# A lockstep top-k search with three tiles on ScalarE, and a pooling input of its own for each half, in a one-core hybrid encoder layer

## The chip, the cores and the metric

The kernel runs on one core of a Trainium2 chip. The metric is the device time of one execution in microseconds. A measured time is the median of several runs; the profile is of one further execution. Engines are named as in the profile: PE (matrix engine; PEld its weight loads), ACT, DVE, POOL, and SP, which here only issues DMAs.

## The reference, cut to what matters

```python
h = rmsnorm(x, norm_g)                      # 1024 tokens, 1024 channels
z = h @ w_in                                # one projection for everything below
# A, pooling: per group of 64 channels a trailing mean over 2/4/8/16 tokens, minus the token
p = win_sum / cnt - v;  a = (p @ w_grp) * scale * silu(pg)
# B, sparse attention: an indexer picks 256 keys for each query
score = sum_h iw[q,h] * relu(iq[q,h] . ik[s]);  score = -inf beyond the query's chunk of 64
sel = top_k(score, 256);  b = softmax(q . k[sel] / 8) @ v[sel] * silu(dg)
# C, forgetting attention: causal, with the bias F[t] - F[s], F = cumsum(log_sigmoid(ff + bf))
c = softmax(q . k / 8 + F[t] - F[s]) @ v * silu(fg)
x = x + concat(a, b, c) @ w_out;  return rmsnorm(x, final_g)
```

## The kernel before, in words

Tokens are cut into 8 tiles of 128. Every float32 product is made of three matmuls on a high and a low part (`mm3`, its matmuls on line 457). `norm` and `idx_proj` make the transposed activations and the indexer's columns tile by tile; `idx_k` makes the indexer's keys, high parts by ACT (line 560) and low parts on partitions 32 to 63 and 96 to 127 by two DVE subtractions (line 562). `idx_tile` makes the scores of tiles 2 to 7 (`sc2` to `sc7`; tile i has (i+1)*128 keys; tiles 0 and 1 have no more than 256 keys and need no search).

The projections that follow are jobs of 24 matmuls, and they are what PE always has at hand. A "half" is 128 output columns for 512 tokens (`chan`, 24 matmuls of 512 columns): fk and fq (keys and queries of C), gp (gate of A), POOL (the pooling input v), gf (gate of C), dk, dq (B) and gd (gate of B). The jobs fv and dv are 384 columns for one token tile (`tokproj`, 24 matmuls of 384 columns). Each job fills one PSUM tile `pj`, of which there are three, and PE can begin a fourth job only when the first has been read out: fk, fq, dk, dq by ACT on line 718 and DVE on 719, fv and dv by ACT 659 and DVE 660, gates by ACT 732 (tanh) and DVE 734, POOL by ACT 1042 into the buffer v.

`pool_tile(m)` runs twice. Its v and two sum buffers s1, s2 come from one ring `pq` of three; windows are added on POOL (line 1049, copy 1053), DVE forms the means (1065, 1067, 1069), PE multiplies (1073), DVE scales the result into a tile `th` (1077), which is stored to DRAM (`mx_p`). The ring `th` has two tiles, which the gates use too (line 731), each stored (`gt_f`) before it is used again.

The top 256 of a row are found by a search for the threshold, bit by bit: a first count and 31 steps, each a count of the scores below the trial value and three small instructions that set the next one (786, 788, 789). Tiles 6 and 7 are counted on ACT (Sign with a summing output, line 768), tiles 2 to 5 on DVE (line 772); the two searches run apart, each with small instructions of its own. `finish` turns thresholds into masks on DVE (813 to 843; with `fix` a tile is counted twice). Until finish has let go of its row buffers there is no place for the attention's tiles `P`, so the first of C's score evictions (line 929) stands behind it.

The order on every engine is made ahead of time by `Plan.schedule`, a list scheduler with planned durations and priorities; each engine then takes its instructions strictly in that order. SP issues all DMAs, in one such order too: loads of keys and queries for the attention (`load_k`, `load_q`) stand in line with stores.

## Time and profile before

| | |
|---|---|
| time, median of 3 runs | 678.64 us (677.1 to 679.01) |
| the profiled execution's own time | 675.91 us |
| its span, first to last instruction | 674.1 us |
| mean granted TensorE clock | 0.983 |
| busy: PE, DVE, ACT, POOL | 631.3, 524.4, 395.9, 202.5 us |

The own time is 1.8 us more than the span. Shares of busy time are means over stages that differ: the indexer up to 135 us, the search with projections up to 293 us, attention with projections up to 600 us, and the output projection.

### The profile page before, as it was taken

How to read it: one execution, taken by the hardware profiler on the slowest of the kernel's cores; microseconds unless marked ns; L12 is line 12 of the kernel's file. 1: busy time of each engine (PE TensorE's matmuls, PEld its weight loads, DVE VectorE, ACT ScalarE, POOL GpSimd, SP SyncE). 2: the span in 40 equal slices, each digit the busy share in tenths (PEclk: the TensorE clock that was granted, in tenths of full speed). 3: DMA queues.
4: the chain of work that ended last, by engine and by line, in shares of the span. 5: the costliest groups of instructions: out<-in, count | busy, mean ns of one | idle time of the engine just before them, and what ended most of it. 6: DMA issues, size and time to landing. Idle time of an engine off the chain costs nothing. (4 is left out here: it accounts for less than half of the span.)

```text
span 674.1 us, 10707 instructions
## 1 busy us (share of the span) xinstructions
PE 631.3 (94%) x3278; PEld 529.4 (79%) x3278; DVE 524.4 (78%) x1363; ACT 395.9 (59%) x904; POOL 202.5 (30%) x218
## 2 busy tenths in 40 slices
PE   7899999999999399879999899999899999989995
PEld 5798777799888399667878688888778777778884
DVE  5978999999999989989997666758576868655322
ACT  5745777566666545531658467778567869731211
POOL 3610324520036512114442442512031435132311
PEclk9999999999999699989999999999899999999999
DMA  7707554640035323744647668569874555266211
GB/s 227 222 1 199 152 167 110 184 132 3 16 97 138 84 104 106 220 144 135 209 156 236 188 171 236 180 189 276 227 233 151 184 175 172 64 196 202 103 63 62
DMA packets 98439, 103.02 MB, mean 153 GB/s; under 512 B 10983, under 2 KB 67399, under 8 KB 98382
## 3 DMA queue, kind: packets, MB, share of 16 engines
q1 hardware_dynamic: 98382, 102.34, 50.8%
q8 instruction: 26, 0.43, 0.3%
q14 instruction: 31, 0.25, 0.1%
HBM read 72.35 MB, written 29.96 MB: 152 GB/s over the span
## 5 line engine op out<-in xcount | busy, mean ns | idle before, releaser
L457 PE MATMUL bank<-RA 128*128 128x512 f32 (+2 forms) x2016 | 492.0, 381 | 16.5 <-ACT FA L1042 10.5
L457 PEld LDWEIGHTS bank<-RA 128*128 128x128 f32 x2016 | 361.2, 190 | 67.6 <-ACT FA L1042 10.9
L957 ACT ACTIVATE RA<-bank 128x512 fp32r<-128x512 f32 (+3 forms) x144 | 67.8, 488 | 62.9 <-PE bank L950 58.8
L772 DVE TENSOR_SCALAR_CACHE_REDUCE FA<-FA 128x384 bf16<-128x384 f32 (+3 forms) x128 | 103.4, 808 | 1.6
L690 POOL TENSOR_TENSOR RA<-FA,RA 128x512 fp32r<-128x512 f32 x44 | 63.8, 1461 | 126.8 <-ACT RA L689 122.0
L768 ACT ACTIVATE FA<-FA 128x896 bf16<-128x896 f32 x64 | 69.8, 1090 | 52.6 <-DVE FA L789 42.9
L929 DVE CUSTOM_DVE_ANT_0 FA<-bank,FA 128x512 f32<-128x512 f32 (+3 forms) x144 | 77.4, 552 | 28.5 <-PE bank L921 9.9
L959 DVE TENSOR_TENSOR RA<-bank,RA 128x512 fp32r<-128x512 f32 (+3 forms) x144 | 77.0, 553 | 23.1 <-ACT RA L957 14.0
L940 ACT ACTIVATE FA<-FA 128x512 f32<-128x512 f32 (+3 forms) x144 | 86.8, 607 | 7.3 <-DVE FA L935 7.2
L950 PE MATMUL bank<-FA 128*128 128x128 f32 x432 | 79.4, 276 | 3.2 <-DVE RA L959 2.2
L950 PEld LDWEIGHTS bank<-FA 128*128 128x128 f32 x432 | 55.7, 141 | 21.3 <-DVE RA L959 5.3
L918 PE MATMUL bank<-RA 128*128 128x512 f32 (+3 forms) x144 | 52.3, 365 | 6.0 <-DVE FA L929 2.9
L602 DVE SCALAR_TENSOR_TENSOR FA<-FA 128x512 f32<-128x512 f32 (+3 forms) x70 | 54.2, 798 | 1.9
L921 PE MATMUL bank<-RA 128*128 128x512 f32 (+3 forms) x144 | 51.1, 361 | 2.6 <-DMA RA<-qk_dq 2.4
L965 PE MATMUL bank<-RA 128*128 128x512 f32 (+3 forms) x144 | 53.4, 375 | 0.0
L963 PE MATMUL bank<-RA 128*128 128x512 f32 (+3 forms) x144 | 49.2, 342 | 0.5 <-ACT RA L957 0.5
L594 ACT ACTIVATE FA<-bank 128x512 f32<-128x512 f32 (+3 forms) x80 | 39.7, 527 | 16.3 <-DVE FA L602 6.8
L925 POOL TENSOR_TENSOR FA<-FA 128x128 f32<-128x128 f32 x48 | 25.6, 541 | 71.2 <-DMA FA<-nf_d 34.9
L918 PEld LDWEIGHTS bank<-RA 128*128 128x128 f32 x144 | 27.1, 189 | 13.3 <-DVE FA L929 7.7
L921 PEld LDWEIGHTS bank<-RA 128*128 128x128 f32 x144 | 27.3, 191 | 6.2 <-DMA RA<-qk_dq 2.6
L963 PEld LDWEIGHTS bank<-RA 128*128 128x128 f32 x144 | 27.3, 190 | 6.3 <-ACT RA L957 2.1
L997 POOL TENSOR_TENSOR FA<-FA 128x512 f32<-128x512 f32 x12 | 16.2, 1347 | 52.9 <-DVE FA L993 27.6
(145 smaller groups left out, 688.1 us busy)
## 6 DMA issues: line engine op xcount, KB each, us to landing
FA<-in_w_in_dram SPq DMA_DIRECT2D x60, 256.0 KB, 3.4
FA<-in_x_dram SPq DMA_DIRECT2D x15, 512.0 KB, 3.6
RA<-qk_fq SPq DMA_DIRECT2D x48, 128.0 KB, 3.9
RA<-qk_dq SPq DMA_DIRECT2D x48, 128.0 KB, 2.8
RA<-qk_dk SPq DMA_DIRECT2D x36, 128.0 KB, 3.3
FA<-in_w_out_dram SPq DMA_DIRECT2D x16, 256.0 KB, 2.8
out_dram<-FA SPq DMA_DIRECT2D x7, 512.0 KB
RA<-qi SPq DMA_DIRECT2D x24, 128.0 KB, 3.0
```

The lines of the kernel that those rows point to most:

```text
L457: M(lambda: nc.tensor.matmul(p()[:, :n], fa(), fb(), start=st, stop=sp), n, keys, [p], pr)
L690: G(lambda raw=raw, s=s: nc.gpsimd.tensor_tensor(Wl()[:, s, :], raw(), f32(Wh()[:, s, :]), op=OP.subtract), 512, [raw, (Wh, kh)], [(Wl, kh ...
L768: A(lambda c=c, i=i, jk=jk, s=s: nc.scalar.activation(jk(), SC[i](), AF.Sign, bias=s(), scale=-1.0, accum_out=cn()[:, c:c + 1]), n, sck(i) ...
L772: V(lambda c=c, i=i, jk=jk, s=s: nc.vector.tensor_scalar(jk(), SC[i](), s(), None, op0=OP.is_lt, op1=OP.add, accum_out=cn()[:, c:c + 1]), ...
L918: M(lambda s=s, k=k, n=n, j=j, hd=hd: nc.tensor.matmul(s()[:, :n], qx()[:, hd, j * 128:j * 128 + 128], k()[:, hd, :n], start=True, stop=Fa ...
L921: M(lambda s=s, k=k, n=n, j=j, hd=hd: nc.tensor.matmul(s()[:, :n], ql()[:, hd, j * 128:j * 128 + 128], k()[:, hd, :n], start=False, stop=T ...
L929: V(lambda s=s, Pt=Pt, n=n, u=u, j=j, mx=mx, bias=bias: nc.vector.tensor_tensor_reduce(Pt()[:, :n], s()[:, :n], bias()[:, u * 512:u * 512 ...
L940: A(lambda Pt=Ps[j][u], n=n, j=j, u=u, hd=hd, nm=nm: nc.scalar.activation(Pt()[:, :n], Pt()[:, :n], AF.Exp, bias=nm()[:, j:j + 1], accum_o ...
L950: M(lambda pt=pt, j=j, Pt=Ps[j][kb // 4], c=kb % 4 * 128: nc.tensor.transpose(pt()[:, j * 128:j * 128 + 128], Pt()[:, c:c + 128], ident()) ...
L957: A(lambda ph=ph, pt=pt, c=c: nc.scalar.activation(ph()[:, c], pt()[:, c], AF.Copy), n, [pt], [ph], pr, psum=True)
L959: V(lambda ph=ph, pl=pl, pt=pt, c=c: nc.vector.tensor_tensor(pl()[:, c], pt()[:, c], f32(ph()[:, c]), op=OP.subtract), n, [pt, ph], [pl], pr)
L963: M(lambda o=o, v=v, ph=ph, c=c, kb=kb: nc.tensor.matmul(o()[:, c], v(), ph()[:, c], start=(kb == 0), stop=False), n, kv + [ph], [o], pr)
```

## The change

- One `search` for all six tiles: tiles 5, 6, 7 are counted on ACT, tiles 2, 3, 4 on DVE, and one set of small instructions on six columns sets all trial values, so all counts of a step wait for the slowest of the step before. `finish` follows for all tiles, with the fix for 5, 6 and 7.
- Each `pool_tile` has a v of its own (tag `pv`, two buffers); the ring `pq` holds only the sums.
- The two small evictions of `idx_proj` (lines 540 and 542) go from DVE to ACT; the bias is added once for all tiles in `forget`.
- `idx_k` makes the low parts with one DVE instruction on all partitions, with a per-partition factor 0 or -1 (`lom`).
- 24 extra small matmuls (`keep_warm`) are queued at the lowest priority, behind the first tile's transposes.

```diff
-    lay("F", f1 + 9 * KB, [("pq", 4160, 3), ("pw", KB, 1)], 1)
+    lay("F", f1 + 9 * KB + 4160, [("pq", 4160, 2), ("pw", KB, 1)], 1)
+    P.tag("pv", "F", 4160, [FSZ - 4160, f1 + 9 * KB], 1)
...
+    def keep_warm(i):
+        for q in range(24):
+            P.op(PE, lambda q=q: nc.tensor.matmul(wu()[:, q % 4 * 128:q % 4 * 128 + 128], identb(), identb(), start=True,
+                                                  stop=True), 0.107, [k_identb, (hT[0], i, 0, "h")], [(wu, q % 4)], 100)
...
-        V(lambda: nc.vector.tensor_tensor(FFA()[:, i * NH:i * NH + NH], p()[:, 296:302], bfb(), op=OP.add), 6,
-          [p, k_bfb], [(cc, "ff", i)], pr)
-        V(lambda: nc.vector.tensor_scalar(iwb()[:, 8 * i:8 * i + 8], p()[:, 288:296], 8.0 ** -0.5, None, op0=OP.mult),
-          8, [p], [(cc, "iw", i)], pr)
+        A(lambda: nc.scalar.activation(FFA()[:, i * NH:i * NH + NH], p()[:, 296:302], AF.Copy), 6, [p],
+          [(cc, "ff", i)], pr, psum=True)
+        A(lambda: nc.scalar.activation(iwb()[:, 8 * i:8 * i + 8], p()[:, 288:296], AF.Copy, scale=8.0 ** -0.5), 8, [p],
+          [(cc, "iw", i)], pr, psum=True)
...
-        for r in (32, 96):
-            V(lambda r=r: nc.vector.tensor_tensor(kk()[r:r + 32], pk()[r:r + 32, :128], f32(kk()[r:r + 32]),
-                                                  op=OP.subtract), 128, [pk, (KI, i)], [(KI, i)], pr)
+        V(lambda: nc.vector.scalar_tensor_tensor(kk(), f32(kk()), lom(), pk()[:, :128], op0=OP.mult, op1=OP.add), 128,
+          [pk, (KI, i), k_lom], [(KI, i)], pr)
...
-        v, s1, s2 = (P.new("pq", [128, W]) for _ in range(3))
+        v, s1, s2 = P.new("pv", [128, W]), P.new("pq", [128, W]), P.new("pq", [128, W])
...
-    sa = search([6, 7], "a")
-    sv = search([2, 3, 4, 5], "v")
-    finish([2, 3, 4, 5], *sv, False)
-    finish([6, 7], *sa, True)
+    on_act = [5, 6, 7]
+    tiles = on_act + [2, 3, 4]
+    finish(tiles, on_act, *search(tiles, on_act))
```

Since the scheduler decides the order, three places show what it made of this. Line numbers of the changed kernel are its own.

ACT at the pooling input: L1042 (L1054 in the changed kernel) evicts a POOL half from a PSUM bank, L768 (L777) is a search count, L689 (L699) a weight split, L659 (L669) the eviction of a dv job. Before:

```order
L768 ACTIVATE FA<-FA 128x896
L768 ACTIVATE FA<-FA 128x1024
L768 ACTIVATE FA<-FA 128x896
L768 ACTIVATE FA<-FA 128x1024
L689 ACTIVATE RA<-FA 128x512 x2
L1042 ACTIVATE FA<-bank_66 128x512
L1042 ACTIVATE FA<-bank_65 128x512
L659 ACTIVATE RA<-bank_71 128x3x2x64
```

Of the change:

```order
L1054 ACTIVATE FA<-bank_71 128x512
L777 ACTIVATE FA<-FA 128x768
L777 ACTIVATE FA<-FA 128x896
L777 ACTIVATE FA<-FA 128x1024
L777 ACTIVATE FA<-FA 128x768
L1054 ACTIVATE FA<-bank_66 128x512
L699 ACTIVATE RA<-FA 128x512 x2
L777 ACTIVATE FA<-FA 128x896
L777 ACTIVATE FA<-FA 128x1024
L669 ACTIVATE RA<-bank_65 128x3x2x64
```

The two evictions of the second pooling half stood together before; they now stand four counts apart, and a step has three counts on ACT instead of two.

ACT at the first gates of C: L732 (L742) is a gate's tanh out of a PSUM bank, L768 (L777) a count. Before:

```order
L768 ACTIVATE FA<-FA 128x1024
L768 ACTIVATE FA<-FA 128x896
L732 ACTIVATE FA<-bank_65 128x512
L768 ACTIVATE FA<-FA 128x1024
L732 ACTIVATE FA<-bank_71 128x512
L732 ACTIVATE FA<-bank_66 128x512
```

Of the change:

```order
L777 ACTIVATE FA<-FA 128x768
L777 ACTIVATE FA<-FA 128x896
L742 ACTIVATE FA<-bank_66 128x512
L777 ACTIVATE FA<-FA 128x1024
L742 ACTIVATE FA<-bank_65 128x512
L777 ACTIVATE FA<-FA 128x768
L777 ACTIVATE FA<-FA 128x896
L742 ACTIVATE FA<-bank_71 128x512
L777 ACTIVATE FA<-FA 128x1024
L699 ACTIVATE RA<-FA 128x512 x2
L742 ACTIVATE FA<-bank_66 128x512
L777 ACTIVATE FA<-FA 128x768
```

Before, one count stood behind the first gate; now seven do (five of them in these rows, two more below), which are all of the last two steps and the last count of the one ahead of them.

DVE where the attention begins: L929 (L941) is C's score eviction, named ISA here, L813 (L825) counts in finish, L734 (L744) and L719 (L729) are evictions of a gate and of a dk half. Before:

```order
L813 TENSOR_SCALAR FA<-FA 128x768
L841 SCALAR_TENSOR_TENSOR FA<-FA 128x640
L832 TENSOR_SCALAR FA<-FA 128x1
L835 TENSOR_SCALAR FA<-FA 128x768
L734 SCALAR_TENSOR_TENSOR FA<-FA,bank_71 128x512
L843 TENSOR_SCALAR FA<-FA 128x640
L837 SCALAR_TENSOR_TENSOR FA<-FA 128x768
L929 ISA FA<-bank_67,FA 128x512
```

Of the change:

```order
L825 TENSOR_SCALAR FA<-FA 128x768
L847 TENSOR_SCALAR FA<-FA 128x768
L729 SCALAR_TENSOR_TENSOR RA<-bank_65,RA 128x512
L844 TENSOR_SCALAR FA<-FA 128x1
L849 SCALAR_TENSOR_TENSOR FA<-FA 128x768
L825 TENSOR_SCALAR FA<-FA 128x896
L941 ISA FA<-bank_67,FA 128x512
```

The gate ahead of the first score eviction was the fifth half of gf; now the second half of dk is evicted ahead of it, so three more projection halves (gf's sixth, two of dk) stand in front of the attention.

## Rows read from the trace of the kernel before

**Rows 1.** Page, busy time, share of the span and instructions of each engine.

```profile
PE 631.3 (94%) x3278; PEld 529.4 (79%) x3278; DVE 524.4 (78%) x1363; ACT 395.9 (59%) x904; POOL 202.5 (30%) x218
```

**Rows 2.** Waits of PE alone: who waited for whom, us, times, longest.

```profile
PE bank L457 <- ACT FA L1042: 10.5, 1, 10.5
PE bank L457 <- DVE FA L734: 3.8, 1, 3.8
...
PE bank L918 <- DMA RA<-qk_fq: 2.0, 1, 2.0
```

**Rows 3.** Timeline, 205 to 250 us: start, duration, instruction, idle before and its releaser.

```profile
220.10 1.05 POOL L1053 COPY FA<-FA 64x1024 f32<-64x1024 f32 x1
...
228.79 1.98 DVE L1065 SCALAR_TENSOR_TENSOR FA<-FA 128x1024 f32<-128x1024 f32 x1
...
232.16 1.09 ACT L1042 ACTIVATE FA<-bank 128x512 f32<-128x512 f32 x2 [3.29 <-DVE FA L789]
...
232.81 15.71 PE L457 MATMUL bank<-RA 128*128 128x384 f32 x75 [10.55 <-ACT FA L1042]
```

**Rows 4.** Windows of 2 us: engines' busy time, then granted clock, DMA share, GB/s.

```profile
230.00:232.00 2.00, 0.00 (x0) 0.00 (x0) 2.00 (x5) 0.00 (x0) 1.89 (x1) 0.50 0.54 122
...
236.00:238.00 2.00, 2.00 (x8) 2.00 (x7) 1.96 (x13) 1.13 (x2) 0.00 (x0) 0.50 0.03 12
238.00:240.00 2.00, 2.00 (x12) 2.00 (x12) 0.84 (x2) 0.28 (x1) 0.00 (x0) 0.98 0.00 0
```

**Rows 5.** Windows: one in the fv jobs, one in the output projection.

```profile
150.00:160.00 10.00, 10.00 (x60) 10.00 (x59) 9.89 (x34) 7.14 (x16) 0.00 (x0) 1.00 0.13 33
...
600.00:660.00 60.00, 60.00 (x267) 49.70 (x266) 22.16 (x42) 12.46 (x18) 17.69 (x13) 1.00 0.37 126
```

**Rows 6.** Window in the first stage.

```profile
20.00:40.00 20.00, 17.61 (x127) 16.28 (x126) 18.52 (x49) 12.69 (x28) 11.37 (x13) 1.00 0.51 148
```

**Rows 7.** Instruction groups by form: busy us, mean ns of one, idle before.

```profile
L768 ACT ACTIVATE FA<-FA 128x1024 bf16<-128x1024 f32 x32 | 36.5, 1141 | 4.1 <-POOL FA L605 3.5
L768 ACT ACTIVATE FA<-FA 128x896 bf16<-128x896 f32 x32 | 33.3, 1039 | 48.5 <-DVE FA L789 42.9 <-DVE FA L788 3.9 <-DVE FA L781 1.7
...
L788 DVE TENSOR_TENSOR FA<-FA 128x2 int32<-128x2 f32 x31 | 10.6, 343 | 1.0 <-ACT FA L768 1.0
```

**Rows 8.** Timeline, ACT in two steps of the search.

```profile
225.42 1.04 ACT L768 ACTIVATE FA<-FA 128x896 bf16<-128x896 f32 x1 [3.92 <-DVE FA L789]
...
226.59 1.15 ACT L768 ACTIVATE FA<-FA 128x1024 bf16<-128x1024 f32 x1
...
235.74 0.19 ACT L768 ACTIVATION_READ_ACCUMULATOR FA<-FA 128x1 f32 x1
...
236.44 1.04 ACT L768 ACTIVATE FA<-FA 128x896 bf16<-128x896 f32 x1 [0.51 <-DVE FA L789]
```

**Rows 9.** Timeline, POOL and DVE at 217 us.

```profile
216.88 1.89 POOL L1049 TENSOR_TENSOR FA<-FA 64x1024 f32<-64x1024 f32 x1
...
217.15 1.72 DVE L788 TENSOR_TENSOR FA<-FA 128x2 int32<-128x2 f32 x2
```

**Rows 10.** Timeline, SP, ACT and PE at the first gates of C.

```profile
267.95 2.39 SPq L360 DMA_DIRECT2D RA<-qk_fk  x4
...
287.38 0.45 SPq L360 DMA_DIRECT2D mx_p<-FA  x1
...
290.86 0.60 ACT L732 ACTIVATE FA<-bank 128x512 f32<-128x512 f32 x1 [3.17 <-DMA mx_p<-FA]
...
292.24 2.98 PE L457 MATMUL bank<-RA 128*128 128x512 f32 x7 [3.75 <-DVE FA L734]
```

**Rows 11.** Timeline, DVE from the first finish to the first score eviction.

```profile
286.57 0.61 DVE L813 TENSOR_SCALAR_CACHE_REDUCE FA<-FA 128x384 bf16<-128x384 f32 x1
...
308.85 0.69 DVE L929 CUSTOM_DVE_ANT_0 FA<-bank,FA 128x512 f32<-128x512 f32 x1 [0.28 <-POOL FA L925]
```

**Rows 12.** Windows of the attention, 310 to 600 us: their sum.

```profile
sum 290.00, PE 279.67 PEld 230.33 DVE 214.38 ACT 197.74 POOL 93.65; mean PE 46.61 PEld 38.39 DVE 35.73 ACT 32.96 POOL 15.61
```

More of the change, by code (lines that the diff above doesn't have):

```diff
@@ L310, in tile_trunk @@
     lay("R", 64 * KB, [("mh", 4 * KB, 2), ("ml", 4 * KB, 2)], 4)
-    NC_ = 672
+    NC_ = 680
     f1 = lay("F", 0, [("c", NC_ * 4, 1), ("raw", 2 * KB, 3), ("th", 2 * KB, 2), ("rs", 32, 4), ("ss", 32, 4),
@@ L392, in tile_trunk @@
     bfb, k_bfb = carve(NH)
+    lom, k_lom = carve(1)
     xt0 = P.new("xt", [128, D])
@@ L417, in tile_trunk @@
     G(lambda: nc.gpsimd.memset(half(), -0.5), 1, [], [k_half])
+    for q in range(4):
+        G(lambda q=q: nc.gpsimd.memset(lom()[32 * q:32 * q + 32], -float(q % 2)), 1, [], [k_lom])
     V(lambda: nc.vector.tensor_scalar(cmask(), iot(), 0.0, NEG, op0=OP.is_gt, op1=OP.mult), 128, [k_iot], [k_cmask],
@@ L622, in forget @@
         v = nc.vector
+        V(lambda: v.tensor_tensor(fa().rearrange("p (i h) -> p i h", h=NH), fa().rearrange("p (i h) -> p i h", h=NH),
+                                  bfb()[:, None, :].to_broadcast([128, NT, NH]), op=OP.add), N, kf + [k_bfb], kf, pr)
         V(lambda: v.tensor_scalar(za(), fa(), -1.0, None, op0=OP.mult), N, kf, [ka], pr)
@@ L744, in tile_trunk, with search @@
     mask = [lambda i=i: maskb()[:, moff[i]:moff[i] + (i + 1) * 128] for i in range(NT)]
-    def search(tiles, a):
-        nq = len(tiles)
-        eng = ACT if a == "a" else DVE
+    def search(tiles, on_act):
+        nq, a = len(tiles), "s"
         t0, _ = carve(nq)
@@ L756, in search @@
             n = (i + 1) * 128
-            G(lambda c=c, n=n: nc.gpsimd.memset(th()[:, c:c + 1],
-                                                float(n - 2 * TOPK if eng == ACT else n - TOPK) + 0.5), 1, [],
+            G(lambda c=c, i=i, n=n: nc.gpsimd.memset(th()[:, c:c + 1],
+                                                     float(n - (2 * TOPK if i in on_act else TOPK)) + 0.5), 1, [],
               [k("th")], 0)
@@ L762, in count @@
         def count(t, kt):
-            for c, i in enumerate(tiles):
+            for c, i in sorted(enumerate(tiles), key=lambda x: x[1] not in on_act):
                 n = (i + 1) * 128
                 s = (lambda: 0.0) if t is None else (lambda c=c: t()[:, c:c + 1])
-                jk = P.new("jka" if eng == ACT else "jkv", [128, n], BF)
-                if eng == ACT:
+                if i in on_act:
+                    jk = P.new("jka", [128, n], BF)
                     A(lambda c=c, i=i, jk=jk, s=s: nc.scalar.activation(jk(), SC[i](), AF.Sign, bias=s(), scale=-1.0,
@@ L771, in count @@
                 else:
+                    jk = P.new("jkv", [128, n], BF)
                     V(lambda c=c, i=i, jk=jk, s=s: nc.vector.tensor_scalar(jk(), SC[i](), s(), None, op0=OP.is_lt,
@@ L793, in search, with finish @@
         return cur, kc, cn, a
-    def finish(tiles, t, kt, cn, a, fix):
+    def finish(tiles, on_act, t, kt, cn, a):
         pr = PR_SEL
         v = nc.vector
-        if fix:
-            nz, knz = carve(len(tiles))
-            V(lambda: v.tensor_scalar(nz().bitcast(I32), t().bitcast(I32), 0x7fffffff, None, op0=OP.bitwise_and), 2,
-              [kt], [knz], pr)
-            V(lambda: v.tensor_scalar(nz(), nz(), 2.0 ** -126, None, op0=OP.is_ge), 2, [knz], [knz], pr)
-            V(lambda: v.tensor_tensor(t(), t(), nz(), op=OP.mult), 2, [kt, knz], [kt], pr)
-        for c, i in enumerate(tiles):
+        na = len(on_act)
+        nz, knz = carve(na)
+        ta = lambda: t()[:, :na]
+        V(lambda: v.tensor_scalar(nz().bitcast(I32), ta().bitcast(I32), 0x7fffffff, None, op0=OP.bitwise_and), na,
+          [kt], [knz], pr)
+        V(lambda: v.tensor_scalar(nz(), nz(), 2.0 ** -126, None, op0=OP.is_ge), na, [knz], [knz], pr)
+        V(lambda: v.tensor_tensor(ta(), ta(), nz(), op=OP.mult), na, [kt, knz], [kt], pr)
+        for c, i in sorted(enumerate(tiles), key=lambda x: x[1]):
+            fix = i in on_act
             n = (i + 1) * 128
@@ L1163, in tile_trunk @@
         norm(i)
+        if i == 0:
+            keep_warm(0)
         idx_proj(i, Wi)
```

2 lines of the change are left out of this document (1 added, 1 removed).

## The prediction

> **What bounds the kernel now.** I read the busy shares first: PE works 631.3 of 674.1 us [rows 1], so the question is where the other 42.8 us lie, and how much of it this change can reach. PE's own waits answer the first half [rows 2]: one wait of 10.5 us on a pooling eviction, one of 3.8 on a gate, one of 2.0 on a key load. DVE with 524 us and ACT with 396 [rows 1] are not the bound by their sums, but in the fv jobs DVE is busy 9.89 of 10 us while PE is busy all of them [rows 5], so the search fills DVE there and its small instructions decide when other work on DVE comes.
>
> The long wait is read from the timeline [rows 3]. PE restarts at 232.81 after 10.55 us idle, when ACT runs two evictions L1042 together at 232.16. These wait for their target, v of the second pooling half, and v has the place of a buffer of the first half, whose last reader on DVE begins with L1065 at 228.79. POOL's last sum for it was done at 221.15, so DVE, in order behind search counts, added 7.6 us. Meanwhile three finished `pj` tiles stood unread. The idle time cost clock too: it is 0.50 in the stall and still 0.50 at 236 to 238, 0.98 after [rows 4]. Those are the two levels 1.2 and 2.4 GHz; 5.2 us of work at the lower one (232.8 to 238) cost 2.6 us. The whole is 13.1 us.
>
> **Pooling buffers of its own.** With `pv`, the second v waits for nothing in the first half. All 13.1 us come back, if PE then finds its evictions on time. It does if the search, which shares ACT and DVE with them, keeps pace.
>
> **The search against PE.** A 512-column matmul takes 60.0/267 = 0.225 us, a half 5.4 us; a 384-column one 10.0/60 = 0.167, an fv or dv job 4.0 us [rows 5]. From fq's last pair of halves to the end of the third gf half PE has 13 halves and 16 such jobs, 134 us, and four L1073 in full float32, which I put at four 512-column matmuls each, 0.9 us (an estimate): 138 us.
>
> A step of the new search on ACT: from a 896 count to the next count 1.17 us, from the start of the 1024 count 1.05 us to its read-out, and from a read-out to the next step's first count 0.70 [rows 8]. A 768 count isn't shown on ACT; 1024 against 896 is 0.10 us more [rows 7], so I take 1.17 less 0.10, 1.07 (bounds: the fit could be off by 0.1). Together 3.99 us, 31 times 124 us. Evictions that stand at a step's end lie inside the 0.70. From the changed order some 23 evictions and splits stand between counts of one step and add about 0.5 us each, 12 us, and pairs of splits 2 us more.
>
> DVE counted four tiles a step and ran two sets of small instructions; with three tiles and one set it no longer sets the pace. But its small instructions now stand in ACT's path. L788 takes 343 ns on average [rows 7], and the reason is visible: two of them that began at 217.15 ended at 218.87, with POOL's addition that began at 216.88 and ended at 218.77 [rows 9]. Some 0.18 us each for L788 and 0.1 for L789 (an estimate by the same excess), 31 times, is 9 us. So the search takes about 147 us, and its first step begins when PE's first half of this stretch is done and read out.
>
> The Trainium skill, in "SBUF — State Buffer", section "SBUF: two separate sides", says that DVE and GpSimd share a port pair as an exclusive lock, held for a whole instruction. Rows 9 agree. By that rule every step whose small instructions meet a POOL addition is lengthened by up to all of it; what that would give is the last rival below.
>
> PE ends the last dv job about 120 us from its start; the 25 steps ahead of that job's eviction end at about 123. That is 3 us late, where three `pj` tiles let PE run two jobs, 8 us, ahead. No stall: price 0 (bounds 0 to 4 lost).
>
> **What stays: the first gates.** The second wait [rows 10] has another cause. PE restarts at 292.24, ACT's tanh waited until 290.86 for a `th` tile, and that for the store of a pooling result, issued by SP at 287.38. Ahead of it SP issues the attention's loads, the first at 267.95, which could start only when the last dv job had released its weights: 30 issues in 19.4 us, 0.65 each. The changed kernel's SP order has the same loads ahead of the same store. From the first load to the tanh stays 22.9 us, to PE's restart 24.3; PE has three halves, two L1073 pairs and two scores until it stands, 19 us. So this wait, the 2.0 us on the key load and the slow clock after it move earlier with everything else and keep their size: price 0 (bounds 6 less, 2 more).
>
> Search counts stand behind that tanh, seven now instead of one. Eleven stand ahead of it and after the last dv; they and two splits take 16 us, so the search reaches the gate with some 5 us to spare and then waits. From the tanh, X, the seven counts with two splits and two step ends end near X + 12. Before, the finish began at 286.57, X - 4.3 [rows 11]. It now begins 16 us later relative to PE.
>
> **The attention.** From the first finish to the first score eviction DVE took 22.3 us [rows 11]; a second count and small instructions of tile 5 add 2, so the first score eviction comes at X + 36.5. PE restarts at X + 1.4 and has six halves and a piece, 33 us, and 2 us of slow clock: X + 36.7. It is covered, but those are three halves more than before, and they are gone as filler later. In the attention PE is busy 279.67 of 290 us, DVE 214, ACT 198 [rows 12]. It is PE's work that sets the length there, and with fewer halves it can be shorter; but it is then denser, and PE's idle 10.3 us should grow. I take 4 us, near the lower end of 0 to 15, since PE at 96% is nearest to no loss.
>
> **The small parts.** In the first 60 us PE has idle time (17.61 of 20 us busy at 20 to 40) while DVE is busy 18.52 [rows 6]. Two small evictions and one of two low-part instructions leave DVE there for each of eight tiles. I take 1.5 us gained, between 4.8 gained (twice the window's 2.4 us of idle time, for the whole first stage) and 1.5 lost: 24 small matmuls, each put at a quarter of a 512-column one, 0.06 us (an estimate), in a stage whose granted clock already reads 1.00 [rows 6], so that keeping PE busy has nothing to keep there. The 16 evictions that ACT takes over are of 6 and 8 columns and lie in its free time, 7.3 of 20 us [rows 6]; without that cover they would delay the projections by no more than what DVE gives up.
>
> **Sum.** Own time 675.9, less 13.1, less 1.5, plus 4: 665.3. The own time is 2.7 us under the median 678.6, so on that scale 668; a measurement can tell about 0.3%, 2 us.
>
> **Rivals.**
> - *The gates' wait goes too* (3.8 and 2.0 us, and 2 of slow clock) and the attention loses nothing: 12 us less, 656. It needs SP to issue the stores early; the order speaks against it.
> - *The attention keeps its own length.* The first score eviction moves from 308.85 to about 313 (X is 14.6 us earlier, 276, plus 36.5). If the remaining 365 us were set by the chain of scores, softmax and transposes and not by PE, the end comes 4 us later than now: 682, slower. For it: fewer halves to fill; against it: DVE 74%, ACT 68% in that stretch. In the forecast the 365 us shrink by 14.5; where they shrink by 4, nothing is left, and halfway, by 7, the time is 675.
> - *The search falls behind, and PE with it.* ACT's evictions stand between counts, so a search slower than planned holds `pj`. Up to 5 us more cost nothing; from there each costs PE one. At 16 us more (a step of 5.3 us all told, not 4.7) the gain is gone, at 22 it is 685. The lock in rows 9 is what would do it, if not 9 but 30 us of POOL's additions hit the steps; against it, in the changed order POOL's additions stand close together in the six steps of the pooling and are rare in the others.
>
> **How the numbers follow.** The forecast has 0.5 (661 to 673), the shorter one 0.14, the attention that keeps its length, wholly or half, 0.2, the slow search 0.1, and 0.06 is none of them. The range for 8 in 10 is 656 to 680. Faster: all of the first two, a third of the third and some of the rest, 0.73; same 0.11; slower 0.16.
>
> **What would show it.** Right: no PE wait on the pooling eviction, and clock 1.00 there; the gates' wait of 4 to 6 us still there, behind SP's loads, some 15 us earlier; ACT steps of 4 to 5 us with the small instructions on DVE between; the first score eviction at 308 to 318 us. Wrong: PE waits on L659's or L1042's successors during the search (the last rival); PE busy under 92% from 310 us on, with waits on softmax or transposes (the second); the stores issued early (the first).

## The result: slower by 0.7%, and the profile after

The changed kernel takes 681.4 us (median of 6 runs, 680.06 to 684.2) against 677.52 us (675.11 to 679.01) for the kernel before beside it: ratio 1.0066, 95% interval 1.0037 to 1.0096. The forecast was 668, with a range of 656 to 680. The profiled execution took 680.85 us, its span 679.0; before, 675.91 and 674.1.

The busy shares of the page answer to [rows 1]. DVE works 49 us less, ACT 34 more, PE 5 more, and PE's 94% are the same 94%.

```profile
PE 636.4 (94%) x3302; PEld 532.3 (78%) x3302; DVE 475.4 (70%) x1188; ACT 429.7 (63%) x984; POOL 199.6 (29%) x222
```

Next PE's waits, which answer to [rows 2]. The wait of 10.5 us on the pooling eviction is gone. The one on the first gate has grown from 3.8 to 5.3. First in the list, by its sum, stands one that the kernel before had for only 0.5 us: matmuls L975 (transposed P times V) waiting for ACT's evictions L969. L930 is a score matmul of the attention.

```profile
PE bank L975 <- ACT RA L969: 6.9, 3, 3.2
PE bank L461 <- DVE FA L744: 5.3, 1, 5.3
PE bank L598 <- ACT FA L602: 3.8, 7, 0.8
PE bank L930 <- DVE FA L941: 3.3, 3, 1.8
```

The timeline shows where the time lies. Columns are start, duration, instruction, idle before and its releaser. L539 is the new small matmul, L598 the index score matmul, L742 a gate's tanh, L825 the finish's first count, L941 a score eviction of the attention.

```profile
26.30 0.67 PE L539 MATMUL bank<-FA 128*128 128x128 bf16 x9
27.64 0.33 PE L567 MATMUL bank<-FA 128*128 128x128 f32 x1 [0.68 <-POOL FA L557]
29.42 0.73 PE L521 MATMUL bank<-FA 128*128 128x128 f32 x4 [1.45 <-DVE RA L526]
...
68.15 0.51 PE L598 MATMUL bank<-RA 128*128 128x384 f32 x2
...
135.31 0.50 PE L598 MATMUL bank<-RA 128*128 128x512 f32 x1 [0.69 <-ACT FA L602]
135.65 106.83 PE L461 MATMUL bank<-RA 128*128 128x512 f32 x539
...
284.77 0.60 ACT L742 ACTIVATE FA<-bank 128x512 f32<-128x512 f32 x1 [5.97 <-DMA mx_p<-FA]
...
286.15 1.22 PE L461 MATMUL bank<-RA 128*128 128x512 f32 x2 [5.34 <-DVE FA L744]
...
298.61 0.61 DVE L825 TENSOR_SCALAR_CACHE_REDUCE FA<-FA 128x384 bf16<-128x384 f32 x1
...
322.54 0.69 DVE L941 CUSTOM_DVE_ANT_0 FA<-bank,FA 128x512 f32<-128x512 f32 x1
...
323.28 0.49 PE L930 MATMUL bank<-RA 128*128 128x256 f32 x1 [1.82 <-DVE FA L941]
...
510.15 0.63 ACT L1110 ACTIVATE RA<-FA 128x512 fp32r<-128x512 f32 x1 [4.60 <-DMA FA<-in_w_out_dram]
510.69 0.96 ACT L969 ACTIVATE RA<-bank 128x512 fp32r<-128x512 f32 x2
...
511.32 0.80 PE L975 MATMUL bank<-RA 128*128 128x512 f32 x1 [2.78 <-ACT RA L969]
...
547.61 1.06 ACT L1129 ACTIVATE RA<-FA 128x1024 fp32r<-128x1024 f32 x1 [5.22 <-DMA FA<-mx_f]
```

The row at 135.65 is the forecast's success: 107 us without a break and at clock 1.00, where [rows 3] had 10.55 us of idle time. Yet the first gate half begins at 286.15 against 292.24 [rows 10], 6.1 us earlier and not 14.6. From there to the end of the span it is 392.85 us against 381.9 before, 11 us more. So there are two losses: one is already there when the gates begin, the other comes after.

The first is seen in two rows of the kernel before: its index scores begin 8.3 us earlier and end 10.1 us earlier than in the changed kernel (68.15 and 135.31).

```profile
59.81 0.51 PE L590 MATMUL bank<-RA 128*128 128x384 f32 x2
...
125.18 0.39 PE L590 MATMUL bank<-RA 128*128 128x512 f32 x1
```

Windows of the changed kernel show PE's clock in both parts, beside [rows 4] (the window, its length, then busy time of PE, PEld, DVE, ACT, POOL, then clock, DMA share, GB/s). After both short stops PE works some microseconds at 0.50, the level of 1.2 GHz: at 30 us behind the small matmuls, and at 512 us behind ACT's wait for a piece of the output weights.

```profile
28.00:30.00 2.00, 0.58 (x5) 0.58 (x6) 2.00 (x5) 0.30 (x2) 1.81 (x2) 0.97 0.86 301
30.00:32.00 2.00, 2.00 (x10) 2.00 (x10) 2.00 (x5) 1.65 (x3) 0.42 (x1) 0.50 0.43 90
...
508.00:510.00 2.00, 0.54 (x3) 0.12 (x1) 0.00 (x0) 0.00 (x0) 0.00 (x0) 1.00 0.90 269
510.00:512.00 2.00, 0.68 (x2) 0.50 (x2) 0.70 (x2) 1.82 (x4) 1.14 (x1) 0.79 1.03 212
512.00:514.00 2.00, 2.00 (x8) 1.56 (x7) 1.64 (x3) 1.90 (x5) 1.18 (x2) 0.50 0.98 294
```

### The profile page after: what moved, and what is told of

The parts are those of the page before. It is cut to its first block, busy times and chain, and to the rows that moved or that the text cites. A ratio compares the mean times of both kernels' runs of the same rounds, so it can differ in the third digit from the quotient of the medians.

```text
span 679.0 us, 10701 instructions
## 1 busy us (share of the span) xinstructions
PE 636.4 (94%) x3302; PEld 532.3 (78%) x3302; DVE 475.4 (70%) x1188; ACT 429.7 (63%) x984; POOL 199.6 (29%) x222
## 4 chain that ended last, share of the span: by engine, by line
PE 58%; DVE 14%; DMA 8%; issue 7%; ACT 7%; SPq 3%; POOL 2%; POOLq 0%; ACTq 0%; DVEq 0%
PE bank L461 41%; PE bank L962 5%; DVE FA L610 4%; SPq L361 3%; PE bank L975 3%; PE bank L977 3%; PE bank L933 3%; PE bank L930 2%; ACT FA L777 2%; DMA FA<-nf_d 1%; ACT FA L952 1%; DVE FA L782 1%; DMA RA<-qk_dq 1%; DMA FA<-in_pool_scale_dram 1%; DMA FA<-in_x_dram 1%
## 5 line engine op out<-in xcount | busy, mean ns | idle before, releaser
L461 PEld LDWEIGHTS bank<-RA 128*128 128x128 f32 x2016 | 362.0, 190 | 63.6 <-DVE FA L744 5.8
L777 ACT ACTIVATE FA<-FA 128x768 bf16<-128x768 f32 (+2 forms) x96 | 99.6, 1037 | 17.0 <-DVE FA L799 10.6
L969 ACT ACTIVATE RA<-bank 128x512 fp32r<-128x512 f32 (+3 forms) x144 | 68.1, 489 | 53.7 <-PE bank L962 49.0
L941 DVE CUSTOM_DVE_ANT_0 FA<-bank,FA 128x512 f32<-128x512 f32 (+3 forms) x144 | 77.7, 550 | 29.6 <-PE bank L962 10.9
L700 POOL TENSOR_TENSOR RA<-FA,RA 128x512 fp32r<-128x512 f32 x44 | 58.6, 1341 | 135.2 <-ACT RA L699 81.3
L971 DVE TENSOR_TENSOR RA<-bank,RA 128x512 fp32r<-128x512 f32 (+3 forms) x144 | 76.7, 552 | 24.9 <-ACT RA L969 20.4
L782 DVE TENSOR_SCALAR_CACHE_REDUCE FA<-FA 128x384 bf16<-128x384 f32 (+2 forms) x96 | 71.1, 741 | 1.5
L962 PEld LDWEIGHTS bank<-FA 128*128 128x128 f32 x432 | 55.8, 141 | 19.8 <-DVE RA L971 4.2
L610 DVE SCALAR_TENSOR_TENSOR FA<-FA 128x512 f32<-128x512 f32 (+3 forms) x70 | 56.3, 822 | 3.9 <-ACT RA L728 0.5
L930 PE MATMUL bank<-RA 128*128 128x512 f32 (+3 forms) x144 | 53.2, 370 | 5.3 <-DVE FA L941 3.3
L975 PE MATMUL bank<-RA 128*128 128x512 f32 (+3 forms) x144 | 50.0, 348 | 6.9 <-ACT RA L969 6.9
L977 PE MATMUL bank<-RA 128*128 128x512 f32 (+3 forms) x144 | 53.8, 379 | 0.2 <-DVE RA L971 0.2
L933 PE MATMUL bank<-RA 128*128 128x512 f32 (+3 forms) x144 | 51.4, 359 | 0.9 <-DMA RA<-qk_dq 0.7
L937 POOL TENSOR_TENSOR FA<-FA 128x128 f32<-128x128 f32 x48 | 27.8, 585 | 65.8 <-DVE FA L941 45.6
L975 PEld LDWEIGHTS bank<-RA 128*128 128x128 f32 x144 | 27.7, 192 | 13.0 <-ACT RA L969 8.9
L930 PEld LDWEIGHTS bank<-RA 128*128 128x128 f32 x144 | 27.2, 189 | 12.8 <-DVE FA L941 8.3
L1130 POOL TENSOR_TENSOR RA<-FA,RA 128x1024 fp32r<-128x1024 f32 x8 | 19.1, 2394 | 59.6 <-ACT RA L1129 49.6
L699 ACT ACTIVATE RA<-FA 128x512 fp32r<-128x512 f32 x44 | 27.2, 629 | 11.9 <-PE bank L461 9.7
```

The costliest lines, as they stand in the source:

```text
L461: M(lambda: nc.tensor.matmul(p()[:, :n], fa(), fb(), start=st, stop=sp), n, keys, [p], pr)
L610: V(lambda rl=rl, w=w, acc=acc, wc=wc: nc.vector.scalar_tensor_tensor(acc(), rl()[:, :w], wc(), acc(), op0=OP.mult, op1=OP.add), w, [rl, ( ...
L777: A(lambda c=c, i=i, jk=jk, s=s: nc.scalar.activation(jk(), SC[i](), AF.Sign, bias=s(), scale=-1.0, accum_out=cn()[:, c:c + 1]), n, sck(i) ...
L782: V(lambda c=c, i=i, jk=jk, s=s: nc.vector.tensor_scalar(jk(), SC[i](), s(), None, op0=OP.is_lt, op1=OP.add, accum_out=cn()[:, c:c + 1]), ...
L930: M(lambda s=s, k=k, n=n, j=j, hd=hd: nc.tensor.matmul(s()[:, :n], qx()[:, hd, j * 128:j * 128 + 128], k()[:, hd, :n], start=True, stop=Fa ...
L933: M(lambda s=s, k=k, n=n, j=j, hd=hd: nc.tensor.matmul(s()[:, :n], ql()[:, hd, j * 128:j * 128 + 128], k()[:, hd, :n], start=False, stop=T ...
```

## The experiments

Each ratio is against runs of the kernel before on the same chip. Diffs show the lines that matter. "Last score" is the start of the last index score matmul, "restart" PE's first matmul after its wait at the first gates of C. The first theory was: some 13 us gained at the pooling, 7 lost in the first stage to the three small edits (small matmuls, index evictions on ACT, key low parts at once), 11 lost in the attention to the lockstep search.

**1. Pooling buffers alone**, on the kernel before.

```diff
-    lay("F", f1 + 9 * KB, [("pq", 4160, 3), ("pw", KB, 1)], 1)
+    lay("F", f1 + 9 * KB + 4160, [("pq", 4160, 2), ("pw", KB, 1)], 1)
...
-        v, s1, s2 = (P.new("pq", [128, W]) for _ in range(3))
+        v, s1, s2 = P.new("pv", [128, W]), P.new("pq", [128, W]), P.new("pq", [128, W])
```

> The kernel before with the pooling buffers alone. Theory (the changed kernel gains some 13 us at the pooling, loses 7 us in the first stage to its three small edits and 11 us in the attention to the one lockstep search): the stall of 10.5 us on the pooling eviction and its slow clock go and little is lost later, 664 to 668 us. Rival (the attention keeps a length of its own, so that work which PE does earlier is lost again later): 674 to 678, no difference that can be told from before.

675.42 us, ratio 0.9954 (0.9924 to 0.9984). 2.8 us faster, where 10 to 14 were expected: PE restarted at the gates only 4.2 us earlier (288.07), having stopped during the search for a fv or dv eviction (2.8 us) and still for a pooling eviction (1.9 us).

**2. Without the small matmuls**, on the changed kernel.

```diff
-        if i == 0:
-            keep_warm(0)
```

> The changed kernel without the 24 small matmuls that keep PE at work. Theory (they stand in PE's order ahead of the index projections and hold one of three projection banks, and that is the 7 us by which the first stage is later): the last qk half ends near 128 us, not 135, and the time is 673 to 676. Rival (the small matmuls lie in idle time, and the index evictions on ACT or the key's low parts are what makes the stage longer): still near 135 us, and 680 to 682.

680.76 us, 1.0045 (1.002 to 1.0069). The last score came at 132.77 and PE's restart 3.5 us earlier, at 282.67, but from there to the end it took 396.2 us, 3.4 more. The theory failed here: this edit alone is not what holds the time up.

**3. Pooling buffers and lockstep search, without the three small edits.** Experiment 2's edit, and on the changed kernel (the second small eviction, the factor `lom` and the bias in `forget` go back as well):

```diff
-        A(lambda: nc.scalar.activation(FFA()[:, i * NH:i * NH + NH], p()[:, 296:302], AF.Copy), 6, [p],
+        V(lambda: nc.vector.tensor_tensor(FFA()[:, i * NH:i * NH + NH], p()[:, 296:302], bfb(), op=OP.add), 6,
...
-        V(lambda: nc.vector.scalar_tensor_tensor(kk(), f32(kk()), lom(), pk()[:, :128], op0=OP.mult, op1=OP.add), 128,
+        for r in (32, 96):
+            V(lambda r=r: nc.vector.tensor_tensor(kk()[r:r + 32], pk()[r:r + 32, :128], f32(kk()[r:r + 32]),
...
```

> Pooling buffers and lockstep search, without the three edits of the first stage. Theory: the first stage is as before (last qk half near 125 to 129 us), the attention loses its 11 us still: 672 to 675. Rival (the first stage is not longer because of these edits, but because the order is made anew): 680 to 682.

665.47 us, 0.9812 (0.9768 to 0.9856), faster than either theory said. The same places of its timeline:

```profile
124.24 0.51 PE L596 MATMUL bank<-RA 128*128 128x512 f32 x1 [0.72 <-ACT FA L600]
...
279.09 3.25 PE L458 MATMUL bank<-RA 128*128 128x512 f32 x7 [4.99 <-DVE FA L740]
...
285.77 0.61 DVE L821 TENSOR_SCALAR_CACHE_REDUCE FA<-FA 128x384 bf16<-128x384 f32 x1
...
289.26 0.61 DVE L847 SCALAR_TENSOR_TENSOR FA<-FA 128x384 bf16<-128x384 f32 x1
...
305.61 0.69 DVE L937 CUSTOM_DVE_ANT_0 FA<-bank,FA 128x512 f32<-128x512 f32 x1
```

Last score 11.1 us earlier than in the changed kernel, PE's restart 7.1, first score eviction 16.9, end of the span 16.7. The lockstep search is no loss; the three small edits together cost some 16 us in the order that the planner made with them. Windows up to the restart, the first of the changed kernel, the second of this one (length, then PE's busy time), tell what its 7.1 us are made of: PE idles 18.9 us in place of 15.6 and works 267.3 in place of 263.5.

```profile
0.00:286.15 286.15, 267.27 (x1399) 230.39 (x1399) 214.04 (x507) 205.93 (x419) 81.72 (x107) 0.99 0.45 132
...
0.00:279.09 279.09, 263.48 (x1375) 227.32 (x1375) 217.34 (x539) 208.05 (x409) 83.62 (x103) 1.00 0.48 135
```

**4. The two old searches**, all other edits kept (`search` and `finish` are those of the kernel before).

```diff
-    on_act = [5, 6, 7]
-    tiles = on_act + [2, 3, 4]
-    finish(tiles, on_act, *search(tiles, on_act))
+    sa = search([6, 7], "a")
+    sv = search([2, 3, 4, 5], "v")
+    finish([2, 3, 4, 5], *sv, False)
+    finish([6, 7], *sa, True)
```

> The changed kernel with the two separate searches of before, all else kept. Theory (the lockstep search ends later against PE, and the attention loses its filler by it): the stretch from the first gate half to the end returns to some 382 us, from 393, and the time is 669 to 672. Rival (the stretch is longer for another reason, each order finding its own stalls and its own drops of the clock): stays near 390, 678 to 682. A third: with DVE as full as before, the 10.5 us come back as waits during the search, 680 or more.

675.49 us, 0.9962 (0.9933 to 0.9992). From the restart to the end 381.8 us, as the theory said, but the restart came at 290.21. The small edits cost nothing here (experiment 1 took as long without them), though the last score was as late as in the changed kernel, 135.60.

**5. ACT told to expect the late loads later**, on the changed kernel: the output weights as below, and the mixed tiles (L1129) alike.

```diff
-                A(lambda raw=raw, s=s, W=W, ws=ws: nc.scalar.activation(W()[:, 0, s, ws], raw(), AF.Copy), 512, [raw],
-                  [(W, c % 4, kh, "h")], pr)
+                P.op(ACT, lambda raw=raw, s=s, W=W, ws=ws: nc.scalar.activation(W()[:, 0, s, ws], raw(), AF.Copy),
+                     t_act(512), [raw], [(W, c % 4, kh, "h")], pr, lag=6.0)
```

> The changed kernel, where the planner is told that ACT's first operation on a loaded piece of the output weights, and on a loaded mixed tile, can come 6 us later than it believes, so that they stand later in ACT's order; nothing else is told. Theory (in the attention ACT waits in order for those two loads, 4.6 and 5.2 us, with evictions of transposed P queued behind it, PE runs dry behind these, and its clock drops): both stalls go, with PE's 6.9 us of waiting on ACT and half of some 7 us of slow clock, 669 to 673 us. Rival (the waits stand in for others, the attention has its own length): 678 to 682.

684.05 us, 1.0072 (1.0044 to 1.01). The rival was right. PE's waits in its profile show that the two stops went (L975 is no longer ahead), and that a key load took their place:

```profile
PE bank L461 <- DVE FA L744: 4.7, 1, 4.7
PE bank L930 <- DMA RA<-qk_dk: 4.4, 1, 4.4
```

So taking those two stops away gained nothing: others came in their place.

**6 and 7. The same work in a slightly other order,** on the kernel of experiment 3 and on the changed one.

```diff
-    SLACK = 0.3
+    SLACK = 0.31
```

> Pooling buffers and lockstep search without the three edits of the first stage, as in the run that took 665.5 us, with one number of the planner at 0.31 in place of 0.30: the same work in a slightly other order. Theory (the gain of that run has causes in the kernel, and the order around it does not matter by more than 2 us): 664 to 668. Rival (each order finds its own stalls, and one of 665 was one of the lucky ones): anywhere from 665 to 680, most likely 670 to 675.

668.22 us, 0.984 (0.9804 to 0.9876): the gain of experiment 3 stays.

> The changed kernel with one number of the planner at 0.31 in place of 0.30: the same work in a slightly other order. Theory (its loss lies in the first stage, 7 us that every such order has, and in two waits of the attention that an order may or may not have): 670 to 682, with the first stage as late as before the number was moved. Rival (the loss belongs to the edits alone): 679 to 683.

693.0 us, 1.0206 (1.0166 to 1.0245), beyond both sides. Last score (134.56) and restart (285.19) were as in the changed kernel; all the difference came later, 405.8 us from restart to end, 13 more than in the changed kernel. In that stretch PE idles 5.3 us more and its work takes 7.7 us longer, with the clock at 0.50 for 30.5 us in place of 13.4.

**8. The small matmuls alone**, added to the kernel of experiment 3.

```diff
+        if i == 0:
+            keep_warm(0)
```

> Pooling buffers and lockstep search with the 24 small matmuls alone, without the other two edits of the first stage. Theory (they make the first stage longer by their own 2 us, by their waits, and by the order in which the projections of two tiles then interleave; in the changed kernel the stage lost some 7 us): last qk half at 131 to 136 us in place of 124, time 671 to 676. Rival (the small matmuls are harmless, as their removal from the changed kernel moved its time by less than 1 us): 664 to 668.

682.44 us, 1.006 (1.0034 to 1.0086): the whole loss again, and more than was expected. The profiled execution was the fastest of its twelve, 677.28 us:

```profile
132.21 0.50 PE L596 MATMUL bank<-RA 128*128 128x512 f32 x1 [0.69 <-ACT FA L600]
...
282.46 2.93 PE L458 MATMUL bank<-RA 128*128 128x512 f32 x6 [4.72 <-DVE FA L740]
...
318.75 0.69 DVE L937 CUSTOM_DVE_ANT_0 FA<-bank,FA 128x512 f32<-128x512 f32 x1
```

So either the small matmuls or the other two edits suffice (experiments 8 and 2), which is why taking one out of the changed kernel changed nothing. This led to the chain theory: last index score, search, finish, first score eviction, end.

**9. A shorter search**, on the changed kernel.

```diff
-        for b in range(30, -1, -1):
+        for b in range(30, 3, -1):
```

> The changed kernel with 27 steps of the search in place of 31; the four lowest bits of each threshold are left out, so the kept set of a row can differ a little. Chain theory (what sets the end is a chain: last index score, some 162 us of search, 20 to 24 us of finish, some 357 us from the first score eviction of the attention to the end; PE only follows it): the finish starts some 19 us earlier, near 279 us, and the time falls until PE's own work bounds it again, 662 to 668 us. Rival (PE and the order of its work set the end, and the search lies beside it): no change, 678 to 684.

666.36 us, 0.9813 (0.9771 to 0.9854). PE restarts where it did in the changed kernel (0.9 us earlier), the first score eviction comes 25 us earlier, and the end 14.3:

```profile
285.28 14.15 PE L461 MATMUL bank<-RA 128*128 128x512 f32 x54 [3.79 <-DVE FA L744]
...
297.28 0.69 DVE L941 CUSTOM_DVE_ANT_0 FA<-bank,FA 128x512 f32<-128x512 f32 x1
```

The search does not lie beside PE.

**10. Index queries first**, on the changed kernel: transposes, evictions, store and loads of the query side get the evictions' precedence.

```diff
     def idx_tile(i):
-        pr = PR_DOT + i * 0.01
+        pr = PR_EV + i * 0.01
...
+        pr = PR_DOT + i * 0.01
         n = (i + 1) * 128
```

> The changed kernel, where the query side of the index tiles (transposes, evictions, store and loads) is given precedence in the planner over the projections, so that index scores can begin while projections still run. Chain theory (the end follows the last index score, which stands at 135.3 us in the changed kernel and at 124 to 125 where the small edits are left out): the last score comes at 122 to 128 us and the time falls with it, 667 to 674 us. Rival (the last score is bound by the work of DVE and ACT ahead of it, not by its start): it stays near 133 to 136 and the time at 678 to 684.

665.87 us, 0.9793 (0.9751 to 0.9834). Scores begin 19 us earlier and end 10.6 us earlier, and with all edits of the change kept the end comes 14.9 us earlier, more than the theory said:

```profile
48.86 0.42 PE L599 MATMUL bank<-RA 128*128 128x384 f32 x1
...
124.69 0.50 PE L599 MATMUL bank<-RA 128*128 128x512 f32 x1 [0.26 <-ACT FA L603]
...
305.73 0.68 DVE L942 CUSTOM_DVE_ANT_0 FA<-bank,FA 128x512 f32<-128x512 f32 x1
```

**11 to 13. No wait at the gates.** The pooling's gates get another ring, on the kernel of experiment 3; then with experiment 10's edit; then all of the change with both.

```diff
-            gt = P.new("th", [128, 512])
+            gt = P.new("rl", [128, 512])
             ld(gt, lambda u=u: GT["p", m, u], 262144, [("gt", "p", m, u)], [gt], pr)
```

> Pooling buffers and lockstep search without the three edits of the first stage (665.5 us), and the gates that the pooling reads in buffers of another ring, so that the first gates of C need not wait for the store of a pooling result. Chain theory (ACT's wait of 5.7 us for that store stands in the search, since counts are queued behind it, and PE's wait of 5.0 beside it): both go, finish and first score eviction come 5 us earlier, 658 to 662 us. Rival (the attention has a length from PE's restart, or another wait stands there instead): 664 to 668.

666.94 us, 0.9817 (0.9772 to 0.9863): the rival. PE's 5 us went, finish and first score came 3.1 and 3.9 us earlier, and the rest took 8.5 longer, 365.2 us.

> As the run with the pooling's gates in another ring, and with the query side of the index tiles ahead of the projections as well. Chain theory: the last index score comes earlier than 124 us, by up to 8, and the end with it until PE's own work bounds it: 650 to 658 us. Rival (PE bounds it already, with 630 us of work in a span of 662): 656 to 662, no more than the other edit alone.

660.88 us, 0.9721 (0.9678 to 0.9765): the rival's range, not the theory's. Experiment 15 below takes the same time without the new ring.

> The changed kernel with all its edits, the query side of the index tiles ahead of the projections, and the pooling's gates in another ring. Theory (the three small edits cost nothing by themselves, only by the order that the planner made around them): as the best run without them, 658 to 664 us. Rival (24 small matmuls and the slow clock behind them stay in front of the last score): 665 to 668.

669.4 us, 0.9845 (0.9803 to 0.9887): the rival, or worse. Its last score came at 124.85, without the small edits (experiment 12) at 120.55. They cost something in this order too; whether by their own work or by the order made around them this run cannot tell.

**14. Lockstep search alone**, on the kernel before: experiment 4's edit the other way round.

> The kernel before with the lockstep search alone, its pooling buffers as they were. Theory of two bounds (the end is the later of the chain through search, finish and attention, and of PE's own order from the first gates on): the chain alone would give some 663, but PE still stops 10 us at the pooling and its slow clock follows, so that it restarts at the gates 13 us later than in the run of 665.5: 671 to 676 us. Rival (only the chain counts, and PE's stop at the pooling is free): 663 to 667. Third (the evictions that wait at the pooling hold counts behind them on ACT, and the search is late by the same 10 us): 676 or more.

667.82 us, 0.9807 (0.9771 to 0.9842), next to the rival's figure, but for a reason that no theory had. PE hardly stops at the pooling, though its buffers are the old ones:

```profile
223.93 12.95 PE L457 MATMUL bank<-RA 128*128 128x384 f32 x73 [1.00 <-ACT FA L1044]
```

**15. Index queries first, on the kernel of experiment 3** (experiment 10's edit).

> Pooling buffers, lockstep search and the query side of the index tiles ahead of the projections; the pooling's gates stay in their old ring. Theory (the earlier last score is what the best run so far gains over 665.5): last score near 120 us, 658 to 662 us. Rival (the wait for the store at the gates takes it back, since it hangs on loads that come when they came): 664 to 667.

660.33 us, 0.9706 (0.9675 to 0.9737): the fastest, with experiment 12.

**16. Index queries first, on the kernel before.**

> The kernel before with the query side of the index tiles ahead of the projections, nothing else. Chain theory: the last score comes near 120 us in place of 125, and finish and end follow, 671 to 675 us. Rival (in this kernel PE's stop at the pooling and DVE's two sets of search steps set the time): 677 to 680.

674.6 us, 0.9922 (0.9892 to 0.9953), the theory's figure and not its way: the last score moved by only 0.9 us, to 124.24, the finish by 7.3, to 279.31, and PE still stopped 8.8 us at the pooling and restarted at 291.32.

**17. Experiment 10 without the small matmuls; 18. experiment 14 with index queries first.**

> The changed kernel with the query side of the index tiles ahead of the projections and without the 24 small matmuls; index evictions on ACT and the key's low parts at once stay. Theory (of the 5.5 us between the changed kernel with that mend, 665.9, and the same without the three small edits, 660.3, the small matmuls are the cause: their own 2 us, PE's stop behind them and the slow clock): last score at 121 to 122 us, 659 to 662 us. Rival (the other two edits, which free DVE, are it, by the order in which projections then stand in pairs): last score near 124 to 125, 664 to 667 us.

661.89 us, 0.975 (0.9724 to 0.9777), as the theory said, last score at 120.53 in place of 124.69.

> The kernel before with the lockstep search and the query side of the index tiles ahead of the projections; pooling buffers as they were. Theory (the pooling buffers are worth 2 us or less once the lockstep search leaves DVE free, since PE's stop at the pooling was 1.0 us with that search alone): 659 to 664 us. Rival (with the search earlier, the pooling's second half meets a fuller DVE and PE stops again): 666 to 672.

668.02 us, 0.9842 (0.9815 to 0.987): the rival. PE stops 4.0 us at the pooling (in an execution of 671.74 us, the slowest of the five). Against experiment 15 the buffers are worth 9 us here (the ratios' difference, 0.0136 of 678); against experiment 3, experiment 14 gives them nothing.

## Why the prediction was wrong

One table sorts the runs in which PE stops at the gates. Times are starts in each profile; the lag is first score eviction less restart, the tail is span less restart.

| kernel | last score | restart | first score | lag | tail |
|---|---|---|---|---|---|
| 9 (shorter search) | 135.14 | 285.28 | 297.28 | 12.0 | 379.4 |
| 16 | 124.24 | 291.32 | 304.67 | 13.4 | 382.7 |
| 1 | 125.56 | 288.07 | 304.00 | 15.9 | 382.5 |
| before | 125.18 | 292.24 | 308.85 | 16.6 | 381.9 |
| 4 | 135.60 | 290.21 | 308.22 | 18.0 | 381.8 |
| 17 | 120.53 | 277.56 | 302.45 | 24.9 | 383.1 |
| 15 | 120.84 | 277.98 | 303.01 | 25.0 | 380.2 |
| 10 | 124.69 | 280.41 | 305.73 | 25.3 | 383.7 |
| 18 | 122.71 | 282.92 | 308.32 | 25.4 | 387.0 |
| 3 | 124.24 | 279.09 | 305.61 | 26.5 | 383.2 |
| 6 | 125.12 | 279.69 | 306.40 | 26.7 | 387.7 |
| 14 | 124.79 | 276.60 | 306.14 | 29.5 | 389.8 |
| 8 | 132.21 | 282.46 | 318.75 | 36.3 | 393.0 |
| after | 135.31 | 286.15 | 322.54 | 36.4 | 392.9 |
| 2 | 132.77 | 282.67 | 319.10 | 36.4 | 396.2 |
| 7 | 134.56 | 285.19 | 321.60 | 36.4 | 405.8 |
| 5 | 135.82 | 286.39 | 324.18 | 37.8 | 395.8 |

Up to a lag of 27 us the tail is 379 to 388, at 36 us and more it is 393 to 406, and experiment 14 lies between. Each row is one execution, and executions of one kernel differ by up to 9.5 us (experiment 1), so the lag tells the group and not the tail to a few us; experiment 7 has the changed kernel's lag and a tail 13 us longer.

What the longer tail is made of is read from windows from the restart to PE's last matmul, the first of the kernel before, the second of the changed kernel:

```profile
292.24:666.60 374.36, 364.03 (x1904) 299.78 (x1904) 254.94 (x642) 215.45 (x551) 117.17 (x114) 0.99 0.57 173
...
286.15:671.60 385.45, 369.15 (x1904) 301.89 (x1904) 259.25 (x675) 222.34 (x563) 117.36 (x114) 0.98 0.56 168
```

The same 1904 matmuls take 11.1 us longer: PE idles 16.3 us in place of 10.3, and its work takes 5.1 us more. The clock is at 0.50 for 13.4 us of it in place of 6.8, which makes 3.3 of these 5.1. Over the table PE idles 7 to 15 us in the rows up to 27 and 15 to 22 in those from 36 on, with the clock at 0.50 for 3 to 11 us and for 13 to 31. In the five rows from 36 on, and in 14 and 18, PE stops ahead of the first score eviction, since a score matmul that needs it is next in order (323.28 in the changed kernel). Between its restart and its next score matmul PE does 148 projection matmuls, 116 in experiment 3 and 71 before: that much filler is used while search and finish still run. Most of the extra idle time is in short stops later in the attention. That they come because less filler was left is the reading that fits; experiment 9 supports it, which shortened the search, left the restart within 0.9 us, and has 8.3 us of idle time and 6.8 of slow clock there. Its order was made anew too, so the lag is not all that it changed.

- **Pooling stall, −13.1.** The stall and its slow clock went, and in experiment 3 PE restarts 13.15 us earlier than before. The size was right for both edits together, but the prediction gave all of it to the buffers. It had itself read that DVE "in order behind search counts" added 7.6 us. Buffers without the lockstep search gain 3 us (experiment 1). The lockstep search with the old buffers leaves 1.0 us of the stop in one order (14) and 4.0 in another (18), and there the buffers are worth 9 us.
- **The small parts, −1.5: the first step that failed.** It had PE's idle time and DVE's share in one window [rows 6] and asked neither when the last index score comes nor what the order becomes. The restart was forecast at X + 1.4 with X at 276, 277.4; it came at 286.15, 7.1 us later than without the small edits (experiment 3). Of these, 3.3 us are idle time and 3.8 work; of the work the 24 small matmuls are some 1.8 us (an estimate: nine take 0.67 at 26.30), and the stretch at 0.50 from 30 us on costs 1.7. Experiments 3, 8 and 2 show that either group of the small edits makes the restart some 3.5 us later and the scores end 8 us later, both groups 7 and 11; 10 shows that most of the scores' delay is the order, since index queries first bring the last score back to 124.69. What remains is smaller: 4.2 us of last score that go with the small matmuls (17), and some 3 us of time by the ratios of 10 and 17, whose intervals overlap.
- **Search, 0, and its step.** From X, the first tanh (284.77), the finish began at X + 13.8 (forecast X + 12) and the first score eviction at X + 37.8 (X + 36.5). Relative to PE's gates this part held, and so did the length: 154.0 us from the first to the last count of tile 7 (142.49 to 296.45), of which ACT waits 6.0 at the gate, so 148 against 147; an undisturbed step takes 3.97 us against 3.99. It was wrong to call the search covered: it is the other half of the bound.
- **First gates, 0.** Right: the wait stayed, 5.3 us. That it is worth anything by itself experiment 11 did not show.
- **Attention, +4: the second step that failed.** It was 11 (392.85 less 381.9). The prediction had the lag nearly right (35.1 us against 36.4), named the reason, three halves fewer as filler, and then took 4 out of 0 to 15 because PE was at 96%. That PE was well filled with a lag of 16.6 says nothing of a lag of 36. PE's idle time grew by 6.0 us, and the clock that falls after its stops, for which this term had nothing, cost 3.3 more. The first score eviction, 322.54, lies outside the prediction's sign of 308 to 318, since the restart came late.
- **The rival "the attention keeps its own length"** gave 682, near the measured time, but not by its own numbers: it had the first score eviction at 313 and up to 365 us behind it, and the trace has 322.54 and 356.5. That its figure comes near is luck. Its sign, PE busy under 92% from 310 us on, did not show: PE is busy 276.3 of 290 us there (95%), since work at half the clock counts as busy.
- **Small slips that moved nothing.** L1073 was put at 0.9 us each; in the trace of before PE goes on 0.46 and 0.57 us after a row of two (281.23, 283.73), so the 138 us are up to 2.6 too many. X + 12 + 22.3 + 2 is X + 36.3, not 36.5, and 1.4 + 33 + 2 is 36.4, not 36.7.

Sum: restart 6.1 us earlier (not 14.6), tail 11 longer (not 4): 4.9 slower in the profiled executions (680.85 against 675.91).

Why the lag is 36.4 in the changed kernel and 26.5 in experiment 3 can be added up. Its last score is 11.1 us later while PE's restart is only 7.1, which is 4.0; from the last score to the finish it takes 1.8 us more; and the finish takes 23.9 us in place of 19.8. In that finish four DVE operations begin just after a POOL operation has begun, two of them here:

```profile
302.09 1.59 POOL L700 TENSOR_TENSOR RA<-FA,RA 128x512 fp32r<-128x512 f32 x1 [6.86 <-ACT RA L699]
...
302.44 1.66 DVE L851 SCALAR_TENSOR_TENSOR FA<-FA 128x384 bf16<-128x384 f32 x1
...
305.47 1.36 POOL L700 TENSOR_TENSOR RA<-FA,RA 128x512 fp32r<-128x512 f32 x1 [1.79 <-ACT RA L699]
...
305.60 1.77 DVE L851 SCALAR_TENSOR_TENSOR FA<-FA 128x512 bf16<-128x512 f32 x1
```

In experiment 3 the same operations (L847) take 0.61 and 0.74. The other two are L851 at 313.11 (1.84 us against 0.88) and L840 at 316.46 (1.20 against 0.22, L836 there). Together that is 4.0 us. This is the pattern of [rows 9] again. By the Trainium skill, "SBUF — State Buffer", section "SBUF: two separate sides", the two engines take a shared port pair in turn for whole instructions; the 1.05 us between the two rows at 302.44 and 289.26 agree. Experiment 3 has one such meeting in its finish (L843 at 295.22, 1.52 us against 0.54) and 0.6 us more of idle time, and the changed kernel has one operation more ahead of its first score eviction (L849 at 319.82, 1.7 us): 4.0 less 1.0 less 0.6 plus 1.7 are the 4.1. Why the order of experiment 7 has so many more stops and so much more slow clock in the attention stays open.

## What to carry to other kernels

Before an engine's idle time is priced, follow the chain that starts the next stage, here last score, search, finish, first score eviction, and ask how much work the busy engine has left until it arrives: up to that cover (a lag of 27 us here) a delay cost little, and some 10 us beyond it cost 10 to 23. Where a planner or scheduler makes the order, an edit of a few microseconds is priced by where the milestones stand in the new order, and a run with the same work in a slightly other order belongs beside every claim of a per cent. Filler work on an engine that is in order ahead of the critical inputs is not free because the engine looks idle.
